# A two-layer decoder step: forget pages loaded as rows, SyncE in written order in the q/k stage, last outputs stored as whole rows

## The chip, the cores and the metric

The kernel runs on one NeuronCore of a Trainium2 chip. A core has five engines with instruction streams of their own: TensorE (PE in the profile, with its weight loads shown apart as PEld), VectorE (DVE), ScalarE (ACT), GpSimd (POOL) and SyncE (SP). SyncE computes nothing here: it issues DMA transfers and reads register values. ScalarE and GpSimd can issue transfers too, each on a queue of its own. The metric is the device time of one execution in microseconds; lower is better. The kernel before took 2829.18 us (median of 3 runs, 2827.18 to 2837.07).

## What is computed

One inference step of a two-layer decoder, for 1024 prompt tokens with 16 meta tokens ahead of them and for 8 decoding requests of 8 tokens each; all 1104 rows go through the same weights. Layer A is an mLSTM (a chunked recurrence with gates), layer B is attention in which every key carries a cumulated log-forget value. After each layer comes a SwiGLU network. Cut to what the change touches:

```python
def mlstm_mixer(xn, C0, n0, m0, lead, w_in, ...):
    p = xn @ w_in                       # q, k, v, output gate, and the small gates gi, gf
    q = heads(p[..., :HK], DK_A) * DK_A ** -0.5
    k = heads(p[..., HK:2 * HK], DK_A)
...
def attend_sample(q, k, v, lf):         # layer B, the 8 decoding requests
    lp = cache_logf[page_table].reshape(Bd, n_pages * PAGE_SIZE, H_B, ...)
    c = jnp.cumsum(jnp.concatenate([lp.astype(f32), lf], axis=1), axis=1)
...
y = rmsnorm(h, prm['norm_final'])       # the last output, y_prompt and y_sample
```

`cache_logf` has pages of 128 positions x 16 heads (8 KB in f32); the page table names 4 pages for each of 8 requests, so 32 pages are read. Everything is f32. A product is made of three passes of rounded halves (high x high, high x low, low x high), so every weight is split once into a high half (a copy on ScalarE that rounds) and a low half (a subtraction on VectorE).

## The kernel before

Work is written in stages that follow one another on TensorE. In stage A the input rows are turned and normalised and the values are made (`values_a`); then comes the **q/k stage** (in `phase_a`), then the recurrence with the output gates between its steps, the output projection and the first feed-forward network (`mlp`, `ffn`), then layer B in the same manner. The last step is in class `Tail`: three tiles of 128 rows remain whose output waits for the last product.

A planner lays out each engine's instruction stream from the program: it takes instructions by priority (written earlier comes first) as soon as by its own clock their data and buffers are there. A block `manual_schedule(engines={...})` takes the named engines out of that: their instructions written inside it keep the written order. The planner may still set others, which are written later, between them. At run time each stream is executed strictly in the order laid out, whatever the planner's clock had thought. In `values_a` (L648) TensorE, SyncE, VectorE and ScalarE are in written order; in the q/k stage before the change only TensorE is (L923).

The q/k stage (`qk_out`, L909 to L920) makes q and k for all rows: 8 blocks m of 128 columns, and in each three groups t of 336, 384 and 384 rows. One pass (m, t) is 24 matmuls (L193 to L195) into one of two PSUM banks, tag `mmA`; ScalarE copies the bank out (L918, tile `stg`) and GpSimd stores it to `qkD`. The passes are counted by x = 3 m + t, from 0 to 23. Between them, by x:

- `load_w` (L233) loads the 512 KB of weights of a block m (L256, tile `wraw`, two buffers) and splits them: high half on ScalarE (L259, `whi`), low half on VectorE (L260, `wlo`), three buffers each. Block 0 was loaded and split in `values_a` (`self.q0`).
- `wo_out` (x = 6, 9, 12, 15, 18) does the same with a block of the output projection's weights, and `wo_keep` stores the halves to `woD` on GpSimd's queue (L875), to be read back in `mlp`.
- `rec_prep` prepares the recurrence's gates. At x = 1 and x = 4 TensorE turns li and lf into rows (L1098, tag `r`, two PSUM banks, three turns each), ScalarE copies them out (L1100), and VectorE scans them (L1102 to L1132). At x = 9 TensorE turns the results back (L1140) and VectorE copies them (L1141).
- `cache_loads` (L997) reads the page table into `ptab` (L1001), and for each of the 32 pages reads its number into a SyncE register (L1008) and loads the page as 128 partitions x 64 bytes (L1010, tile `cp`). One step of it loads 4 pages; a step is taken after each x from 0.
- `cache_prep` (x = 14): 4 turns on TensorE (L1021), a copy with the sign changed on ScalarE (L1022), a scan along the positions on VectorE (L1024), and 8 stores to `csE` on GpSimd's queue (L1027). Layer B reads them much later.

In the functions below `wo_fetch` (L850) and `wo_split` (L859) are what `values_a` uses already: a load alone, and later the split alone.

In `Tail.out` (L2061), for each of three tiles, VectorE and ScalarE scale one half of 512 columns each out of PSUM into places of `net.H` that are 128 columns wide and 4 apart, and SyncE stores each half (L2072): six stores of 256 KB.

Of the kernel before, what the change touches and what calls it, by code (L numbers as in the profile page):

```python
# [8 lines left out]
F32 = mybir.dt.float32  # L9
F32R = mybir.dt.float32r  # L10
I32 = mybir.dt.int32
AF = mybir.ActivationFunctionType
ALU = mybir.AluOpType
# [4 lines left out]
P = 128  # L18
D = 1024
KT = D // P  # L20
NB, NQ = 8, 8
# [6 lines left out]
TT = [(0, T0)] + [(T0 + P * i, T0 + P * (i + 1)) for i in range(SEQ // P)]  # L28
# [10 lines left out]
HB, DH = 16, 64  # L39
DFF = 2816  # L40
NF = DFF // P
PAGE, NPG = 128, 4
PAST = PAGE * NPG
# [835 lines left out]
@_add(Net)  # L879
def phase_a(self, vt):  # L880
    nc, I, O = self.nc, self.I, self.O
    w_in = I["w_in_a"][0]
    qkD = self.dram.tile([8, P, T], F32, name="qkD")
    ogD = self.dram.tile([8, P, T], F32, name="ogD")
    v = lambda i: vt[:, i * HA * (DV + 1) : (i + 1) * HA * (DV + 1)].rearrange("p (h d) -> p h d", h=HA)
    with ExitStack() as c3:
        kp = c3.enter_context(self.pool("kA"))
        tm = kp.tile([P, NT, 104], F32, name="tmA")
        den = kp.tile([P, NT, HA], F32, name="den")
        ssq = kp.tile([P, NT, HA], F32, name="ssqA")  # L890
        self.C = [kp.tile([P, 4, DV + 1], F32, name=f"C{a}") for a in range(3)]
        gates = kp.tile([P, NT, 16], F32, name="gates")
        self.fin = (tm, den, ssq)
        for i in range(NT):
            nc.gpsimd.memset(v(i)[:, :, DV : DV + 1], 1.0)
        nc.gpsimd.memset(gates, 0.0)
        nc.gpsimd.memset(tm[:, 0, :], 0.0)
        nc.gpsimd.memset(den, 1.0)
        nc.gpsimd.memset(ssq, 1.0)
        st = c3.enter_context(self.pool("stA", bufs=3))  # L900
        self.woD, self.held = [], []
        self.values_a(v, kp, gates, w_in, c3)
        pp = c3.enter_context(self.pool("ppA", bufs=2, space=PSUM))

        def wo_out():
            m = len(self.woD)
            self.wo_keep(*self.load_w([I["w_out_a"][0][:, m * P : (m + 1) * P]]))

        def qk_out():  # L909

            for m in range(8):
                wh, wl = self.load_w([w_in[:, m * P : (m + 1) * P]]) if m else self.q0
                for t, (t0, t1) in enumerate(TG):
                    n = t1 - t0
                    ps = pp.tile([P, 512], F32, name=self.uid("mmA"), tag="mmA")
                    self.fm_cols(ps[:, :n], wh, wl, self.XG[t])
                    s = st.tile([P, GL], F32, name=self.uid("stg"), tag="stg")
                    nc.scalar.activation(s[:, :n], ps[:, :n], AF.Copy, scale=DK ** -0.5 if m < 4 else 1.0)  # L918
                    nc.gpsimd.dma_start(qkD[m, :, t0:t1], s[:, :n])
                    yield  # L920

        with self.pool("rowsA") as rp, self.pool("rowsAp", bufs=2, space=PSUM) as rpp, \
                self.pool("cp") as cp, self.tc.manual_schedule(engines={mybir.EngineType.PE}):  # L923
            pages = self.cache_loads(cp)
            prep = self.rec_prep(kp, gates, rp, rpp)
            next(prep)
            for x, _ in enumerate(qk_out()):
                if x in (1, 4, 9):
                    next(prep, None)
                next(pages, None)  # L930
                if x == 14:
                    self.cache_prep(*self.cache, rpp, "r")
                if x % 3 == 0 and 5 < x < 21:
                    wo_out()

        def gates_out():

            get = lambda m, later=None: self.load_w([w_in[:, (16 + m) * P : (17 + m) * P]], later=later)
            ws = [get(0)]
            later = []  # L940
            for m in range(8):
                wh, wl = ws[m]
                for t, (t0, t1) in enumerate(TG):
                    n = t1 - t0
                    ps = pp.tile([P, 512], F32, name=self.uid("mmA"), tag="mmA")
                    xh, xl = self.XG[t]
                    if t == 1 and m < 7:
                        ws.append(get(m + 1, later if m else None))
                    for k in range(KT):
                        if k == 6 and later:  # L950
                            later.pop()()
                        self.mm3(ps[:, :n], wh[:, k, :], wl[:, k, :], xh[:, k, :], xl[:, k, :], k == 0, k == KT - 1)
                        if k == KT - 1:
                            s = st.tile([P, GL], F32, name=self.uid("stg"), tag="stg")
                            nc.scalar.activation(s[:, :n], ps[:, :n], AF.Sigmoid)
                            nc.gpsimd.dma_start(ogD[m, :, t0:t1], s[:, :n])
                        yield

        left = {t: list(range(HA)) for t in range(3)}
        left[-1] = [None]  # L960

        def heads(pp, tag, op=None, some=None):

            ready, used = [], []
            todo = [(t, h) for t in (0, 1, 2) for h in left[t]][:some]

            def ahead():
                if todo:
                    t, h = todo.pop(0)
                    og = op(self.uid("ogc")) if callable(op) else op.pop(0)  # L970
                    nc.gpsimd.dma_start(og[:, : TG[t][1] - TG[t][0]], ogD[h, :, TG[t][0] : TG[t][1]])
                    ready.append(og)

            def gate(t):
                if not left[t]:
                    return False
                while todo and (len(ready) < 3 if callable(op) else op):
                    ahead()
                if t < 0:
                    return False  # L980
                og = ready.pop(0)
                self.gate_head(t, left[t].pop(0), v, og, pp, tag)
                if not callable(op):

                    used.append(og)
                    if len(used) > 1:
                        op.append(used.pop(0))
                return True
            return gate

        self.recurrence(kp, self.rec, v, qkD, gates_out(),
                        lambda places: heads(pp, "mmA", places, 10))
    return heads


@_add(Net)
def cache_loads(self, cp):  # L997

    nc, I = self.nc, self.I
    self.csE = self.dram.tile([NB, P, PAST], F32, name="csE")  # L1000
    nc.sync.dma_start(self.ptab, I["page_table"].rearrange("b n -> (b n)").unsqueeze(0))  # L1001
    self.pages = []
    a, b = (cp.tile([P, 2 * PAST], F32, name=f"cp{x}") for x in range(2))
    lp = a[:, : NPG * NB * HB].rearrange("p (n b h) -> p n b h", n=NPG, b=NB)
    for b_ in range(NB):
        for n in range(NPG):
            j = b_ * NPG + n
            v = nc.sync.value_load(self.ptab[0:1, j : j + 1], min_val=0, max_val=I["cache_k"].shape[0] - 1)  # L1008
            self.pages.append(v)
            nc.sync.dma_start(lp[:, n, b_, :], I["cache_logf"][bass.DynSlice(v, 1)].rearrange("a p h -> (a p) h"))  # L1010
        yield
    self.cache = lp, a[:, PAST:], b[:, :PAST], b[:, PAST:]


@_add(Net)
def cache_prep(self, lp, cs, lt, on, pp, tag):

    nc = self.nc
    ps = pp.tile([P, 512], F32, name="csps", tag=tag)
    for n in range(NPG):  # L1020
        nc.tensor.transpose(ps[:, n * P : n * P + P], lp[:, n].rearrange("p b h -> p (b h)"), self.ident)  # L1021
    nc.scalar.activation(lt, ps, AF.Copy, scale=-1.0)  # L1022
    nc.gpsimd.memset(on, 1.0)
    nc.vector.tensor_tensor_scan(cs, on, lt, 0.0, ALU.mult, ALU.add)  # L1024
# [977 lines left out]
class Tail:  # L2002
# [57 lines left out]

    def out(self, x, lo, hi):  # L2061
        net, i = self.net, DONE[3][x]
        nc, t0, t1 = net.nc, *TT[i]
        for g, ps in enumerate((lo, hi)):
            o = net.H[:, 4 * g : 4 * g + 4, t0:t1]
            y, rr = ps.rearrange("p (k n) -> p k n", k=4), self.r[:, 1, x : x + 1]
            if g:
                nc.scalar.activation(o, y, AF.Copy, scale=rr)
            else:
                nc.vector.scalar_tensor_tensor(out=o, in0=y, scalar=rr, in1=net.sq[:, :512].rearrange(  # L2070
                    "p (k n) -> p k n", k=4), op0=ALU.mult, op1=ALU.mult)
            nc.sync.dma_start(net.O["y_prompt"][0, (i - 1) * P : i * P, g * 512 : g * 512 + 512].rearrange(  # L2072
                "p (k n) -> p k n", k=4), o)

    def finish(self, acc, groups):
        net = self.net
# [963 lines left out]
```

## Time and profile before

| | us |
|---|---|
| median of 3 runs | 2829.18 (2827.18 to 2837.07) |
| profiled execution, its own time | 2829.72 |
| its span (first to last instruction) | 2828.0 |
| TensorE busy in the span | 2761.9 (98%) |
| VectorE, ScalarE, GpSimd busy | 1800.4, 1177.3, 836.0 |
| mean granted TensorE clock | 0.994 |

The page shows one profiled execution. Busy times are sums over the span; matmuls are pipelined, so that a busy TensorE is not one at its peak, and where it is slowed by its clock only the granted clock tells so. "DMA" is the mean busy share of 16 DMA engines. In a timeline each row has the start, the length, the engine, the source line, the operation, what it writes and reads, how many were merged, and in brackets how long the engine had stood idle before and what ended that. A row of "who waited" has the waiting group, the releasing one, the sum in us, the number of times and the longest. Rows of a table by windows have the window, its length, each engine's busy time with its number of instructions, the granted clock, the DMA share and GB/s.

### The profile page before, as it was taken

The page shows a single profiled execution, that of the slowest core. Times are in us where ns is not written, and L with a number is a line of the kernel's source. Part 1 is how long each engine was busy: PE and PEld are TensorE (multiplying, and loading weights), DVE is VectorE, ACT ScalarE, POOL GpSimd, SP SyncE. Part 2 cuts the span into 40 slices and gives each one's busy share as a digit, 9 for nine tenths or more (in the row PEclk, how much of TensorE's full clock was granted, in tenths as well). Part 3 has the DMA queues.
Part 4 walks back from the last instruction along what each step waited for, and adds up shares of the span by engine and source line. Part 5 has one row for each costly group of instructions (what it writes and reads, how often), then busy time and mean ns, then how long its engine had stood idle before and what let it go on. Part 6 is the DMA issues. An engine that isn't in the chain of part 4 may idle for free. (4 is left out here: it accounts for less than half of the span.)

```text
span 2828.0 us, 60538 instructions
## 1 busy us (share of the span) xinstructions
PE 2761.9 (98%) x23543; PEld 2650.3 (94%) x23543; DVE 1800.4 (64%) x4025; ACT 1177.3 (42%) x2299; POOL 836.0 (30%) x1313
## 2 busy tenths in 40 slices
PE   8999999999999999999999999999999999999998
PEld 8989889999999999999999888677999999999998
DVE  4632566888887765563455444777388888766556
ACT  5422453432322334443444445777343223323345
POOL 3122233132232332124453202544313223323111
PEclk9999999999999999999999999999999999999999
DMA  6666547245554375545444676442524555527556
GB/s 196 171 196 162 144 125 255 90 143 165 176 167 148 112 243 174 195 145 171 139 172 132 237 279 226 154 143 86 157 83 128 175 176 164 161 90 239 178 191 215
DMA packets 439001, 474.03 MB, mean 168 GB/s; under 512 B 41422, under 2 KB 365258, under 8 KB 437690
## 3 DMA queue, kind: packets, MB, share of 16 engines
q1 hardware_dynamic: 387522, 320.78, 36.8%
q0 software_dynamic: 43808, 143.17, 15.3%
q10 hardware_dynamic: 7384, 6.22, 0.7%
q8 instruction: 185, 3.03, 0.5%
q14 instruction: 102, 0.84, 0.1%
HBM read 322.84 MB, written 147.21 MB: 166 GB/s over the span
## 5 line engine op out<-in xcount | busy, mean ns | idle before, releaser
L1611 PE MATMUL m<-xh,slot 128*128 128x276 f32 x2752 | 541.3, 290 | 1.8 <-ACT fs L1640 1.8
L1611 PEld LDWEIGHTS m<-xh,slot 128*128 128x128 f32 x2752 | 440.4, 188 | 3.6 <-ACT fs L1640 2.2
L1611 PE MATMUL m<-xl,slot 128*128 128x276 f32 x1376 | 397.4, 289 | 0.0
L1611 PEld LDWEIGHTS m<-xl,slot 128*128 128x128 f32 x1376 | 259.1, 188 | 0.0
L193 PE MATMUL tmps<-slot,xh 128*128 128x256 f32 (+2 forms) x864 | 243.1, 281 | 0.0
L195 PE MATMUL tmps<-slot,xl 128*128 128x256 f32 (+2 forms) x864 | 240.6, 278 | 0.0
L194 PE MATMUL tmps<-slot,xh 128*128 128x256 f32 (+2 forms) x864 | 240.5, 278 | 0.0
L272 DVE TENSOR_TENSOR slot<-slot,slot 128x1024 fp32r<-128x1024 f32 x124 | 162.9, 1314 | 60.7 <-ACT slot L271 59.2
L271 ACT CAST slot<-slot 128x1024 fp32r<-128x1024 f32 x124 | 129.6, 1046 | 141.2 <-PE m L1611 111.7
L194 PEld LDWEIGHTS tmps<-slot,xh 128*128 128x128 f32 (+1 forms) x864 | 159.2, 184 | 0.1
L195 PEld LDWEIGHTS tmps<-slot,xl 128*128 128x128 f32 (+1 forms) x864 | 158.6, 184 | 0.0
L193 PEld LDWEIGHTS tmps<-slot,xh 128*128 128x128 f32 (+1 forms) x864 | 158.4, 183 | 0.2
L193 PE MATMUL mmA<-xh,whi 128*128 128x384 f32 (+1 forms) x384 | 135.1, 352 | 0.0
L194 PE MATMUL mmA<-xl,whi 128*128 128x384 f32 (+1 forms) x384 | 127.9, 333 | 0.0
L195 PE MATMUL mmA<-xh,wlo 128*128 128x384 f32 (+1 forms) x384 | 127.7, 333 | 0.0
L272 DVE TENSOR_TENSOR slot<-vA,slot 128x1024 fp32r<-128x1024 f32 (+1 forms) x59 | 82.2, 1396 | 32.6 <-ACT slot L271 31.5
L272 DVE TENSOR_TENSOR slot<-Ht,slot 128x1024 fp32r<-128x1024 f32 (+1 forms) x59 | 81.4, 1382 | 32.3 <-ACT slot L271 31.1
L271 ACT CAST slot<-Ht 128x1024 fp32r<-128x1024 f32 (+1 forms) x59 | 61.0, 1037 | 96.8 <-PE m L1611 92.9
L271 ACT CAST slot<-vA 128x1024 fp32r<-128x1024 f32 (+1 forms) x59 | 60.8, 1035 | 95.5 <-PE m L1611 90.5
L1715 DVE TENSOR_TENSOR ws<-ws 128x128 f32<-128x128 f32 x264 | 93.8, 355 | 8.9
L2862 ACT ACTIVATE s<-s,nb 128x272 f32<-128x272 f32 (+7 forms) x126 | 98.9, 786 | 0.0
L2897 ACT COPY th<-tp 128x768 f32<-128x768 f32 (+1 forms) x80 | 73.6, 920 | 53.7 <-PE tp L2889 30.5
(805 smaller groups left out, 8668.8 us busy)
## 6 DMA issues: line engine op xcount, KB each, us to landing
ws<-in_w_down SPq DMA_DIRECT2D x176, 128.0 KB, 2.8
sD<-ws SPq DMA_DIRECT2D x176, 128.0 KB, 2.3
slot<-sD SPq DMA_DIRECT2D x40, 512.0 KB, 4.2
slot<-in_w_gate_up SPq DMA_DIRECT2D x36, 512.0 KB, 3.9
kp<-in_cache_k SPq DMA_DIRECT2D x32, 512.0 KB, 6.7
vp<-in_cache_v SPq DMA_DIRECT2D x32, 512.0 KB, 5.1
vA<-in_w_gate_up SPq DMA_DIRECT2D x26, 512.0 KB, 4.4
Ht<-in_w_gate_up SPq DMA_DIRECT2D x26, 512.0 KB, 3.9
```

What stands on the lines that cost most here:

```text
L193: mm(ps, sh, mh, start=first, stop=False)
L194: mm(ps, sh, ml, start=False, stop=False)
L195: mm(ps, sl, mh, start=False, stop=last)
L271: self.nc.scalar.copy(hi, src)
L272: self.nc.vector.tensor_tensor(out=lo, in0=src, in1=hi.bitcast(F32), op=ALU.subtract)
L1611: nc.tensor.matmul(u.ps[h, b], w[p][:, k], x[q][:, k], start=first and k == i == 0, stop=k == 3 and i == 2, skip_group_check=True)
L1715: tt(out=o, in0=a, in1=b, op=ALU.subtract)
L2862: nc.scalar.activation(ss[z, u], ss[z, u], AF.Exp, bias=nb[:, z : z + 1], accum_out=sm[:, u, z : z + 1])
L2897: nc.scalar.copy(th.rearrange("p x z (u h q) -> p h (x z u) q", h=2, q=64)[:, :, :n], pt[:, :, :n])
```

## The change

Three things are edited.

**Pages.** `cache_loads` loads a page as one row of 8 KB into one partition of a tile `pg` (32 rows used), instead of 128 pieces of 64 bytes. `cache_prep` then first turns the 16 heads' columns on TensorE (16 turns of 32 rows into 128, out of steps of 16 elements) into one PSUM bank, VectorE copies the bank with its order changed to `lp`, and the 4 turns follow as before. It comes at x = 12 instead of 14. The pages' steps begin at x = 1.

**SyncE.** In the q/k stage SyncE is in written order as well as TensorE. Weights come by `wo_fetch` and `wo_split`: the load of q/k block m + 1 is written at (m, 0), ahead of its matmuls, that of output block m + 2 at (m, 1) for m from 1 to 5; the splits are written at (m, 2), and at (m, 0) for the output block. The written order on SyncE is so: block 1; page table; pages of 8; block 2; pages of 4; output block 3; pages of 8; block 3; pages of 4; output block 4; pages of 8; block 4, and so on without pages. Reading the page numbers into registers stands in that order too, each ahead of its page.

**Last outputs.** `Tail.out` writes both halves of a tile side by side into one row of `net.H` (1024 columns) and stores the tile with one transfer of 512 KB with rows of 4 KB; the third of the three is issued by ScalarE instead of SyncE.

```diff
@@ -879,6 +879,7 @@
 @_add(Net)
 def phase_a(self, vt):
     nc, I, O = self.nc, self.I, self.O
+    E = mybir.EngineType
     w_in = I["w_in_a"][0]
     qkD = self.dram.tile([8, P, T], F32, name="qkD")
     ogD = self.dram.tile([8, P, T], F32, name="ogD")
@@ -902,36 +903,37 @@
         self.values_a(v, kp, gates, w_in, c3)
         pp = c3.enter_context(self.pool("ppA", bufs=2, space=PSUM))
 
-        def wo_out():
-            m = len(self.woD)
-            self.wo_keep(*self.load_w([I["w_out_a"][0][:, m * P : (m + 1) * P]]))
-
         def qk_out():
 
             for m in range(8):
-                wh, wl = self.load_w([w_in[:, m * P : (m + 1) * P]]) if m else self.q0
+                wh, wl = self.q0
                 for t, (t0, t1) in enumerate(TG):
+                    if t == 0 and m < 7:
+                        self.wo_fetch(w_in[:, (m + 1) * P : (m + 2) * P])
+                    elif t == 1 and 0 < m < 6:
+                        self.wo_fetch(m + 2)
                     n = t1 - t0
                     ps = pp.tile([P, 512], F32, name=self.uid("mmA"), tag="mmA")
                     self.fm_cols(ps[:, :n], wh, wl, self.XG[t])
                     s = st.tile([P, GL], F32, name=self.uid("stg"), tag="stg")
                     nc.scalar.activation(s[:, :n], ps[:, :n], AF.Copy, scale=DK ** -0.5 if m < 4 else 1.0)
                     nc.gpsimd.dma_start(qkD[m, :, t0:t1], s[:, :n])
+                    if t == 2 and m < 7 or t == 0 and len(self.held) > 1:
+                        self.wo_split()
                     yield
 
         with self.pool("rowsA") as rp, self.pool("rowsAp", bufs=2, space=PSUM) as rpp, \
-                self.pool("cp") as cp, self.tc.manual_schedule(engines={mybir.EngineType.PE}):
+                self.pool("cp") as cp, self.tc.manual_schedule(engines={E.PE, E.SP}):
             pages = self.cache_loads(cp)
             prep = self.rec_prep(kp, gates, rp, rpp)
             next(prep)
             for x, _ in enumerate(qk_out()):
                 if x in (1, 4, 9):
                     next(prep, None)
-                next(pages, None)
-                if x == 14:
+                if x:
+                    next(pages, None)
+                if x == 12:
                     self.cache_prep(*self.cache, rpp, "r")
-                if x % 3 == 0 and 5 < x < 21:
-                    wo_out()
 
         def gates_out():
 
@@ -1000,25 +1002,32 @@
     self.csE = self.dram.tile([NB, P, PAST], F32, name="csE")
     nc.sync.dma_start(self.ptab, I["page_table"].rearrange("b n -> (b n)").unsqueeze(0))
     self.pages = []
-    a, b = (cp.tile([P, 2 * PAST], F32, name=f"cp{x}") for x in range(2))
-    lp = a[:, : NPG * NB * HB].rearrange("p (n b h) -> p n b h", n=NPG, b=NB)
-    for b_ in range(NB):
+    raw = cp.tile([P, PAGE * HB], F32, name="pg")
+    for b in range(NB):
         for n in range(NPG):
-            j = b_ * NPG + n
+            j = b * NPG + n
             v = nc.sync.value_load(self.ptab[0:1, j : j + 1], min_val=0, max_val=I["cache_k"].shape[0] - 1)
             self.pages.append(v)
-            nc.sync.dma_start(lp[:, n, b_, :], I["cache_logf"][bass.DynSlice(v, 1)].rearrange("a p h -> (a p) h"))
+            nc.sync.dma_start(raw[n * NB + b : n * NB + b + 1, :],
+                              I["cache_logf"][bass.DynSlice(v, 1)].rearrange("a p h -> a (p h)"))
         yield
-    self.cache = lp, a[:, PAST:], b[:, :PAST], b[:, PAST:]
-
-
-@_add(Net)
-def cache_prep(self, lp, cs, lt, on, pp, tag):
+    self.cache = raw, cp.tile([P, PAST], F32, name="lp")
+
+
+@_add(Net)
+def cache_prep(self, raw, lp, pp, tag):
 
     nc = self.nc
+    J = NB * NPG
+    ps = pp.tile([P, 512], F32, name="pgps", tag=tag)
+    for h in range(HB):
+        nc.tensor.transpose(ps[:, h * J : h * J + J], raw[:J].rearrange("j (t h) -> j t h", h=HB)[:, :, h],
+                            self.ident[:J, :J])
+    nc.vector.tensor_copy(lp.rearrange("p (j h) -> p j h", h=HB), ps.rearrange("p (h j) -> p j h", h=HB))
+    cs, lt, on = (raw[:, x * PAST : (x + 1) * PAST] for x in range(3))
     ps = pp.tile([P, 512], F32, name="csps", tag=tag)
     for n in range(NPG):
-        nc.tensor.transpose(ps[:, n * P : n * P + P], lp[:, n].rearrange("p b h -> p (b h)"), self.ident)
+        nc.tensor.transpose(ps[:, n * P : n * P + P], lp[:, n * P : n * P + P], self.ident)
     nc.scalar.activation(lt, ps, AF.Copy, scale=-1.0)
     nc.gpsimd.memset(on, 1.0)
     nc.vector.tensor_tensor_scan(cs, on, lt, 0.0, ALU.mult, ALU.add)
@@ -2060,17 +2069,11 @@
 
     def out(self, x, lo, hi):
         net, i = self.net, DONE[3][x]
-        nc, t0, t1 = net.nc, *TT[i]
-        for g, ps in enumerate((lo, hi)):
-            o = net.H[:, 4 * g : 4 * g + 4, t0:t1]
-            y, rr = ps.rearrange("p (k n) -> p k n", k=4), self.r[:, 1, x : x + 1]
-            if g:
-                nc.scalar.activation(o, y, AF.Copy, scale=rr)
-            else:
-                nc.vector.scalar_tensor_tensor(out=o, in0=y, scalar=rr, in1=net.sq[:, :512].rearrange(
-                    "p (k n) -> p k n", k=4), op0=ALU.mult, op1=ALU.mult)
-            nc.sync.dma_start(net.O["y_prompt"][0, (i - 1) * P : i * P, g * 512 : g * 512 + 512].rearrange(
-                "p (k n) -> p k n", k=4), o)
+        nc, rr = net.nc, self.r[:, 1, x : x + 1]
+        y = net.H[:, x, :D]
+        nc.scalar.activation(y[:, 512:], hi, AF.Copy, scale=rr)
+        nc.vector.scalar_tensor_tensor(out=y[:, :512], in0=lo, scalar=rr, in1=net.sq[:, :512], op0=ALU.mult, op1=ALU.mult)
+        (nc.scalar if x == 2 else nc.sync).dma_start(net.O["y_prompt"][0, (i - 1) * P : i * P], y)
 
     def finish(self, acc, groups):
         net = self.net
```

## The prediction

> **What bounds the kernel now.** I read the page's slices first, then who TensorE waited for in the q/k stage, and a table of windows of that stage.
>
> ```profile
> PE   8999999999999999999999999999999999999998
> ```
>
> ```profile
> core 0: us, PE busy (x) PEld busy (x) DVE busy (x) ACT busy (x) POOL busy (x), PEclk, DMA share, GB/s
> 126.72:245.00 118.28, 111.01 (x671) 109.03 (x669) 39.36 (x76) 33.46 (x53) 27.43 (x58) 0.96 0.67 195
> 155.55:158.70 3.15, 3.15 (x11) 2.98 (x12) 3.15 (x10) 0.78 (x2) 1.11 (x2) 0.50 0.61 168
> 158.70:161.85 3.15, 3.15 (x20) 3.15 (x20) 3.15 (x3) 0.10 (x1) 0.00 (x0) 1.00 0.23 66
> 177.17:181.04 3.87, 3.67 (x27) 3.13 (x25) 1.43 (x3) 1.22 (x2) 0.55 (x1) 1.00 1.08 391
> 182.50:185.91 3.41, 3.41 (x13) 3.41 (x12) 1.23 (x1) 0.00 (x0) 0.00 (x0) 0.51 0.70 183
> 186.00:189.41 3.41, 3.41 (x21) 3.41 (x21) 0.00 (x0) 0.49 (x1) 0.55 (x1) 1.00 0.53 159
> ```
>
> ```profile
> PE rps L1098 <- ACT lf L1100: 6.8, 1, 6.8
> PE wps L1144 <- DVE tmA L1141: 0.2, 1, 0.2
> ```
>
> TensorE bounds the kernel nearly everywhere. The q/k stage (126.7 to 245) leaves it idle for 7.3 us of 118.3, almost all in one wait of 6.8 us, and twice its clock is halved for about 3 us. Who held the wait up is told by the timelines of TensorE, ScalarE and SyncE:
>
> ```profile
> 147.96 0.78 PE L1098 MATMUL rps<-ident,lf_tm 80*8 80x80 f32 x6
> 155.55 0.80 PE L1098 MATMUL rps<-ident,lf_tm 128*8 128x128 f32 x3 [6.80 <-ACT lf L1100]
> 156.00 0.67 PE L193 MATMUL mmA<-xh,whi 128*128 128x384 f32 x1
> ```
>
> ```profile
> 153.75 1.04 ACT L259 CAST whi<-wraw 128x1024 fp32r<-128x1024 f32 x1 [9.25 <-DMA wraw<-in_w_in_a]
> 154.70 0.48 ACT L918 ACTIVATE stg<-mmA 128x384 f32<-128x384 f32 x1
> 155.08 0.78 ACT L1100 COPY lf<-rps 8x336 f32<-8x336 f32 x2
> ```
>
> ```profile
> 122.86 2.64 SPq L256 DMA_DIRECT2D wraw<-in_w_in_a  x2
> 130.71 0.37 SPq L256 DMA_DIRECT2D wraw<-in_w_out_a  x1
> 131.34 18.28 SPq L1010 DMA_DIRECT2D cp<-in_cache_logf  x32
> 149.74 0.39 SPq L256 DMA_DIRECT2D wraw<-in_w_in_a  x1
> ```
>
> Read from below: SyncE issued all 32 pages in one piece, 18.28 us, and block 3's weight load behind them, at 149.74. ScalarE had that block's split next in its stream and stood 9.25 us for it, although TensorE's pass x = 4 had been over since 147.96. Behind it queued the copy of that pass and the first copy of lf, whose PSUM bank the third turn of lf needs. TensorE did not need block 3 itself for another three passes.
>
> **The change part by part.** The sum is made against the profiled execution, 2829.72 us (span 2828.0 and 1.7 around it), 0.5 us above the median of 2829.18.
>
> **1. The wait.** If it goes, 6.8 us go. Behind it 11 matmuls fill 3.15 us at a clock of 0.50 where the next 3.15 us hold 20; those from 156.00 to 158.70 would take about half of 2.7 us: 1.3 us more. **−8.1 us**; bounds 0 and −8.1.
>
> Whether it goes hangs on when block 3 lands and where the planner puts its split. The register reads are a cost here that the stage did not have: the planner had set them into the values stage, and now they stand in SyncE's written order, each ahead of its page.
>
> ```profile
> L1008 SPq TENSOR_LOAD <-ptab x32: 262/275/1086, 12.7 to 47.3; - x32
> L1008 SPq FUSED_REGOPS  x32: 147/147/181, 13.2 to 47.6; - x32
> L1008 SPq SEQ_ASSERT  x32: 18/18/33, 13.4 to 47.8; - x32
> L1001 SPq DMA_DIRECT2D ptab<-in_page_table x1: 289/289/289, 8.2 to 8.2; - x1
> DMA to landing us min/median/max: 1.5/1.7/4.0
> DMA to landing us min/median/max: 4.2/4.8/5.5
> ```
>
> (The first landing row is the pages', the second the weights'.) A page costs 0.57 us of issuing (18.28 / 32) and 0.44 for its number (0.275 + 0.147 + 0.018): 1.01 us; one row of 8 KB in place of 128 pieces I price the same, since the page table, one piece, still takes 0.29 to issue. Block 3 now stands behind block 1, the page table (0.29 and its landing, 1.7 as a page), 20 pages, block 2 and one output block: 122.9 + 0.4 + 2.0 + 20.2 + 0.8 = 146.3, landed 4.8 later at 151. That is only 2 to 3 us earlier than the 153.75 of today, and with the page table's 4.5 us of the start (8.2 to 12.7) it isn't earlier at all. So the gain doesn't come from an earlier load. It comes from ScalarE's order: the split must be laid out behind the copies that are due at 148 to 149. Today the planner had reckoned with 32 cheap issues; now its clock has to count 20 register reads as well, which it set one after another into SyncE's idle stretches before, so it prices them as something. I take it that the split falls behind the lf copies. A split that then waits till 151 delays only the copy of x = 5, due at about 153. Nothing else is late: block 4, behind all 32 pages (122.9 + 2.4 + 32.3 + 2.0), is issued at about 160 and landed at 165, and x = 12, which needs it, begins two passes behind the turns of x = 9, which begin at 177 today and 169 then; a pass of 24 matmuls is 3.8 us at 20 in 3.15.
>
> **2. The turns.** TensorE has 16 more of them, out of 32 rows. The nearest row:
>
> ```profile
> L1140 PE MATMUL tps<-ident,stk x9: 251/252/309, 177.2 to 178.1; 104*128 104x104 f32 x8, 104*80 104x104 f32 x1
> 177.17 1.18 PE L1140 MATMUL tps<-ident,stk 104*80 104x104 f32 x9
> L1141 DVE COPY tmA<-tps x3: 263/592/592, 177.5 to 178.4; 128x416 f32<-128x416 f32 x2, 80x104 f32<-80x104 f32 x1
> L1021 PE MATMUL csps<-ident,cp x4: 270/272/272, 203.1 to 203.4; 128*128 128x128 f32 x4
> ```
>
> 9 in 1.18 us are 0.13 each, so 16 take **+2.1 us** on TensorE itself; bounds 1.6 (weights alone, at 0.1) and 4.2 (twice, for columns read at steps of 16).
>
> **3. The copy between the turns.** The 4 old turns read what VectorE copies after the 16 new ones, so TensorE, whose order is written, stands meanwhile, and pass x = 13 behind it. 128x416 took 0.592, so 128x512 takes 0.73, with 0.2 on each side for the hand-over (TensorE waited 0.2 for L1141 above): **+1.1 us** if VectorE is free. Bounds 0.7 (the copy alone) and 6.5, if VectorE's stream has a weight split ahead that waits for a store, as here:
>
> ```profile
> 198.80 1.23 DVE L260 TENSOR_TENSOR wlo<-wraw,whi 128x1024 fp32r<-128x1024 f32 x1 [5.41 <-DMA woD<-wlo]
> ```
>
> **4. The clock.** 16 turns, the copy and 4 turns (0.6 us) are 3.8 us of light work. The windows show what followed 3.87 us of it at x = 9 (turns and tiny products): 3.41 us at clock 0.51, with 13 matmuls where 21 fit, a loss of 1.3 us. **+1.3 us**; bounds 0 and 1.3. The Trainium skill, "TensorE: Matmul & The Clock Gate", Part 4, says that turns do not count as busy for the gate; by it the 3.8 us is idle to the gate and the loss sure, without it only the 1.1 us wait would count and the loss could be nothing.
>
> **5. The tail.** What is left of the kernel after TensorE's last product:
>
> ```profile
> 2819.96 4.12 SPq L2072 DMA_DIRECT2D out_y_prompt<-Ht  x6
> L2070 DVE SCALAR_TENSOR_TENSOR Ht<-fin,tr,sq 128x512 f32<-128x512 f32 x3 | 2.1, 744 | 0.1
> 24.00:30.00 6.00, 5.13 (x45) 4.97 (x44) 4.76 (x11) 5.02 (x12) 0.86 (x1) 1.00 1.02 393
> 2821.00:2826.50 5.50, 0.00 (x0) 0.00 (x0) 0.38 (x1) 0.09 (x1) 0.00 (x0) 0.51 0.99 281
> DMA packets 654, 2.36 MB, mean 393 GB/s; under 512 B 78, under 2 KB 79, under 8 KB 653
> DMA packets 3169, 1.58 MB, mean 122 GB/s; under 512 B 96, under 2 KB 3168, under 8 KB 3168
> ```
>
> The 16 DMA engines are full (0.99) from 2821.0 to 2826.5, at 281 GB/s, in pieces under 2 KB (the second packet row). In the stretch of the first packet row, 24 to 30, nearly all were 2 to 8 KB and the same engines, as full, moved 393. The 1.57 MB in rows of 4 KB then take 4.0 us. They start later, since a store needs both halves: about 2820.1 instead of 2819.96. The tiles are ready each 0.7 us and need 1.3 to move, so the engines don't starve, and the issue on ScalarE's queue saves nothing that is on the path: **−1.4 us**; bounds −1.6 and +0.2 (no faster rate). The Trainium skill, "DMA: Bandwidth & Descriptors", Specifications, puts line rate at 512 B and more; by it the rate would stay and the tail come out at +0.2, but the two windows speak against it. It is a rival below.
>
> **6. The values stage** loses SyncE's 32 register reads.
>
> ```profile
> 27.80 1.06 PE L732 MATMUL xps<-ident,xin 128*128 128x128 f32 x8 [0.86 <-DMA xin<-in_x_prompt]
> 32.36 0.52 PE L193 MATMUL tmps<-whi,xh 128*80 128x272 f32 x1 [1.99 <-ACT whi L271]
> ```
>
> The input loads between 17 and 33 stand among them. I take **−0.5 us**, half of the wait of 0.86 for an input; bounds 0 and −2.9 (both waits).
>
> At no cost: GpSimd's queue issues the same transfers, with the stores to `csE` two passes earlier, where TensorE waits for none of them (the only waits of the stage are those above), and the weights' splits are the same instructions.
>
> The sum is −8.1 + 2.1 + 1.1 + 1.3 − 1.4 − 0.5 = −5.5 us: 2829.7 − 5.5 = 2824.2, 0.5 less on the scale of the median; I say **2824**.
>
> **The rivals.**
>
> *The wait stays (slower).* The planner still lays block 3's split ahead of the lf copies, which decides it. As block 3 lands at 151 to 154, ScalarE stands as today and part 1 is worth nothing: −5.5 + 8.1 = +2.6, 2832.3 us. For it: the landing by the sum above has hardly moved. Against it: the split is written at x = 8 and the copies at x = 4, and only a clock that runs ahead of SyncE's real pace lets it in.
>
> *A new wait in place of the old.* VectorE's copy of the pages stands behind a weight split that waits for its store (5.41 + 1.23 above): TensorE stands up to 5.4 us longer at x = 12, 2829.6 us, as before. For it: VectorE waited so at 198.8, close to where x = 12 ends. Against it: the copy is written before the next split.
>
> *The stores are no faster.* Issue or memory limits them, not the size of a piece: 1.6 us more, 2825.8.
>
> *The planner lays out other streams anew.* Engines not in written order may change places anywhere behind. The largest idle sum that it could touch is layer B's:
>
> ```profile
> 1580.00:1980.00 400.00, 380.99 (x4773) 304.36 (x4771) 227.38 (x1008) 254.54 (x494) 134.13 (x339) 1.00 0.56 192
> ```
>
> 19 us of 400. All of it gone would make 2805, as much again 2843. Nothing in the trace speaks for either.
>
> **How the numbers follow.** Forecast 0.47, the wait stays 0.16, the new wait 0.12, stores no faster 0.05, other streams 0.20 (gain and loss even). A measurement of this kernel can tell about 0.5% from no change, 14 us: below 2815.0 or above 2843.3. Only the last case reaches that far, with half of its 0.20 each way at most; a forecast with its best bounds (turns 1.6, copy 0.7, no clock loss, −2.9 in the values stage) gives 2819.4, and the first rival with a late copy and no faster stores 2839. So faster 0.10, same 0.80, slower 0.10. The range takes in these bounds but for the far ends of the last case: 2815 to 2836.
>
> **What would show it.** Right: no wait of TensorE for ScalarE's lf copies; a row of 16 turns, a gap of about 1.1 us and 4 turns between x = 12 and 13; clock 0.5 for 3.4 us after it, none at 156; the last three stores moving at about 390 GB/s for 4 us; register reads on SyncE from 123 to 165. Wrong: a wait of 5 us or more at L1098 (first rival) or at L1021's turns (second); stores at 281 GB/s; or gains and losses beyond 245 us that no part names.

## The result and the profile after

The changed kernel takes 2849.47 us (median of 5 runs) where the kernel before took 2832.84 beside it (5 runs): ratio 1.0068, 95% interval 1.0057 to 1.008. It is slower by 0.7%. The profiled execution is 2848.91 us with a span of 2846.9, against 2829.72 and 2828.0 before: 18.9 us more of span.

Start times of the same TensorE instruction in the two traces (in pass x; m is the block) tell where they went; the lag is after minus before:

| instruction | before | after | lag | in between |
|---|---|---|---|---|
| last lf turn begins | 155.55 | 149.35 | -6.2 | wait for lf gone |
| x = 5 under way | 158.39 | 150.90 | -7.5 | its half-clock gone |
| x = 6 under way (m = 2) | 163.33 | 166.85 | +3.5 | waits of 8.65 and 0.33, half-clock |
| x = 9 under way (m = 3) | 176.56 | 186.35 | +9.8 | waits of 2.51 and 0.88, half-clock |
| x = 12 begun (m = 4) | 191.37 | 205.75 | +14.4 | waits of 1.56 and 0.69; the half-clock behind the turns of x = 9 lasts 6.8 us (clock 0.50 and 0.58 from 191.27 to 198.07), twice as long as before |
| x = 13 begun | 194.74 | 214.40 | +19.7 | 16 and 4 turns, wait of 2.73 |
| x = 13 under way | 196.30 | 217.26 | +21.0 | half-clock |
| near the end | 2757.69 | 2777.97 | +20.3 | 18.7 to 22.4 all along |

All of the loss arises between 150 and 220 us. First the view of who TensorE waited for in 126.7 to 245 (sum, times, longest), after the window row of the same stretch (the row of before had a clock of 0.96 and 671 matmuls):

```profile
126.70:245.00 118.30, 100.05 (x548) 95.63 (x547) 40.13 (x77) 29.31 (x46) 24.98 (x55) 0.88 0.56 169
```

```profile
PE mmA L193 <- ACT whi L271: 12.7, 3, 8.6
PE csps L1030 <- DVE lp L1026: 2.7, 1, 2.7
PE mmA L195 <- DVE wlo L272: 1.9, 3, 0.9
PE rps L1107 <- ACT lf L1109: 0.3, 1, 0.3
162.66 0.65 PE L193 MATMUL mmA<-xh,whi 128*128 128x336 f32 x1 [8.65 <-ACT whi L271]
```

The wait that bound the kernel before, 6.8 us for lf, is 0.3. In its place TensorE waits three times for a weight block's split (`whi`, `wlo`), the first time for 8.65 us ahead of x = 6 (last line), and once for the copy between the turns. ScalarE's and SyncE's timelines show why, for block 2:

```profile
148.89 0.78 ACT L1109 COPY lf<-rps 8x336 f32<-8x336 f32 x2
155.13 1.12 ACT L1136 ACTIVATE stk<-mA 8x1104 f32<-8x1104 f32 x1 [4.78 <-DVE mA L1119]
156.27 0.49 ACT L919 ACTIVATE stg<-mmA 128x384 f32<-128x384 f32 x1
159.01 1.12 ACT L1133 ACTIVATE wA<-wA 8x1104 f32<-8x1104 f32 x1 [2.24 <-DVE wA L1131]
160.41 1.12 ACT L1143 ACTIVATE stk<-bA 8x1104 f32<-8x1104 f32 x1 [0.29 <-DVE bA L1141]
161.56 1.04 ACT L271 CAST whi<-wraw 128x1024 fp32r<-128x1024 f32 x1
```

```profile
129.52 9.26 SPq L1011 DMA_DIRECT2D pg<-in_cache_logf  x8
138.88 0.41 SPq L854 DMA_DIRECT2D wraw<-in_w_in_a  x1
...
145.88 9.60 SPq L1011 DMA_DIRECT2D pg<-in_cache_logf  x8
163.89 0.41 SPq L854 DMA_DIRECT2D wraw<-in_w_in_a  x1
```

Block 2's load was issued at 138.88. Its split at 161.56 has no bracket: ScalarE did not wait for the data. It had stood idle for 4.78 and 2.24 us for VectorE's scans just before, with the split laid out behind the three exps that need those scans. So the weight was late by its place in ScalarE's stream. The delay then reaches SyncE: two raw buffers hold the blocks, so block 3's load, which SyncE reached at 155.5 (145.88 + 9.60), went out at 163.89, when block 2's split had been done.

The tail came out near its forecast. From the start of the last group of products to the end of the span it takes 8.17 us (2838.73 to 2846.9) in place of 9.44 (2818.56 to 2828.0):

```profile
2840.29 0.99 SPq L2076 DMA_DIRECT2D out_y_prompt<-Ht  x2
2841.62 0.36 ACTq L2076 DMA_DIRECT2D out_y_prompt<-Ht  x1
2841.00:2845.00 4.00, 0.00 (x0) 0.00 (x0) 0.53 (x1) 0.25 (x1) 0.00 (x0) 0.73 0.98 393
```

393 GB/s with the DMA engines full (0.98), as the prediction had it, against 281 before.

### The profile page after: what moved, and what is told of

Same layout as the page of the kernel before. It is cut to its first block, busy times and chain, and to the rows that moved or that the text cites. A ratio compares the mean times of both kernels' runs of the same rounds, so it can differ in the third digit from the quotient of the medians.

```text
span 2846.9 us, 60569 instructions
## 1 busy us (share of the span) xinstructions
PE 2772.1 (97%) x23559; PEld 2657.5 (93%) x23559; DVE 1797.6 (63%) x4026; ACT 1176.5 (41%) x2299; POOL 833.9 (29%) x1313
## 5 line engine op out<-in xcount | busy, mean ns | idle before, releaser
L193 PE MATMUL mmA<-xh,whi 128*128 128x384 f32 (+1 forms) x384 | 138.1, 360 | 12.8 <-ACT whi L271 12.7
## 6 DMA issues: line engine op xcount, KB each, us to landing
ws<-in_w_down SPq DMA_DIRECT2D x176, 128.0 KB
sD<-ws SPq DMA_DIRECT2D x176, 128.0 KB
```

The costliest lines, as they stand in the source:

```text
L193: mm(ps, sh, mh, start=first, stop=False)
```

## The experiments

Two theories for the late splits. **Theory 1**: the planner, which lays out ScalarE's and VectorE's streams, reckons the rows of 8 KB as slow, so it takes every weight behind them on SyncE for late and sets its split late. **Theory 2**: the register reads, now in SyncE's written order, make the loads really late. A third, that the written order of SyncE as such does it, goes with the second. The lag in the table is that of the same TensorE instruction against before, at 300 us of before, in the profiled runs; the changed kernel's lag there is 21.5. Differences of 1.5 us between lags are no finding: between 258 and 261 us the kernel before has a stretch of half clock that `tail`, for one, does not have, and that alone moves its lag by 1.4.

| kernel | median us | ratio to before, 95% | lag at 300 | TensorE's waits over 1 us, 126.7 to 245 |
|---|---|---|---|---|
| tail | 2828.41 | 0.9984 to 1.0004 | -1.3 | lf 7.2 |
| pages | 2833.89 | 1.0004 to 1.0024 | +3.9 | VectorE's tmA 4.0, whi 1.6 |
| order | 2833.89 | 1.0001 to 1.0021 | +3.0 | stg 8.3 |
| free | 2833.38 | 1.0005 to 1.0024 | +4.4 | whi 1.6 twice, stg 2.0, lp 1.2 |
| early | 2842.92 | 1.0032 to 1.0063 | +16.8 | whi 3.7, 1.6, 1.6, wlo 3.8, lp 2.8 |
| late | 2851.08 | 1.0063 to 1.0096 | +24.6 | page rows 10.2 |
| reads | 2824.31 | 0.9974 to 0.9992 | -4.4 | li 1.5 |
| shift | 2820.19 | 0.996 to 0.9982 | -8.8 | none |
| turns | 2823.64 | 0.9972 to 0.9991 | -3.2 | none |
| moved | 2840.96 | 1.0028 to 1.0058 | +13.2 | page rows 12.8, whi 1.6 |
| hand | 2839.25 | 1.0018 to 1.005 | +10.5 | stg 6.1 and 2.3, lf 1.3, li 1.2 |
| hand2 | 2829.52 | 0.9993 to 1.0013 | +2.8 | stg 2.7 (at 234), lf 1.3, li 1.2 |

**tail**: the kernel before with the new `Tail.out` alone.

> The kernel before with the new last stores alone. If a store's rate hangs on the size of its pieces, the last 1.57 MB move at 390 to 410 GB/s and the end comes 1.4 us earlier: span 2826.6 in place of 2828.0, all of it after 2819, nothing changed in the q/k stage. If the tail also costs something that the trace of the changed kernel hides elsewhere, the ratio comes out above 1.

The q/k stage is as before (wait of 7.2 us for lf). The tail took 8.22 us (2819.98 to 2828.2), 1.2 less than before, moving 397, 397 and 426 GB/s in the three full microseconds. The span, 2828.2, did not fall, because TensorE was 1.4 us later at 2809 by small differences that came and went through both layers; the interval holds both 1 and 0.9995.

**order**: the changed kernel with the functions `cache_loads` and `cache_prep` of before.

```diff
-            nc.sync.dma_start(raw[n * NB + b : n * NB + b + 1, :],
-                              I["cache_logf"][bass.DynSlice(v, 1)].rearrange("a p h -> a (p h)"))
+            nc.sync.dma_start(lp[:, n, b_, :], I["cache_logf"][bass.DynSlice(v, 1)].rearrange("a p h -> (a p) h"))
```

> The changed kernel with the pages loaded and turned as before (64-byte pieces, 4 turns): SyncE's written order, the loads and splits of weights apart, the register reads in line and the new stores stay. Theory 1 (the planner prices the loads of whole rows dearly, takes the weights behind them for late and lays their splits late in ScalarE's stream): without rows the splits stand early, no wait of TensorE for whi over 1 us in the q/k stage, and the old wait for lf is gone: 2820 to 2824 us where the kernel before takes 2830. Theory 2 (the register reads on SyncE make the weights late): the waits at blocks 2 and 3 stay, 2838 us or more. Theory 3 (SyncE's written order as such): the same 2838 or more.

Neither was right as a whole. Waits for whi are gone, as theory 1 had it, with the reads still in line. But the time is not 2822: a new wait of 8.3 us for a copy of PSUM (`stg`) stands at 165.4. ScalarE's and SyncE's timelines of this kernel:

```profile
140.90 1.05 ACT L271 CAST whi<-wraw 128x1024 fp32r<-128x1024 f32 x1 [4.79 <-DMA wraw<-in_w_in_a]
149.36 0.47 ACT L1102 COPY lf<-rps 8x384 f32<-8x384 f32 x1 [0.21 <-PE rps L1100]
162.68 1.04 ACT L271 CAST whi<-wraw 128x1024 fp32r<-128x1024 f32 x1 [12.85 <-DMA wraw<-in_w_in_a]
```

```profile
128.68 8.32 SPq L1012 DMA_DIRECT2D cp<-in_cache_logf  x8
137.11 0.40 SPq L854 DMA_DIRECT2D wraw<-in_w_in_a  x1
153.30 0.39 SPq L854 DMA_DIRECT2D wraw<-in_w_in_a  x1
```

With pieces of 64 bytes block 2 is split at 140.90, not at 161.56, although its load went out at nearly the same time (137.11, not 138.88). Now block 3's split stands early too, right behind the lf copies, and its load goes out at 153.30 only: ScalarE stands 12.85 us for it, the same kind of wait as before the change, two passes further on (ahead of x = 7, not x = 5). So theory 1 holds for block 2, and the reads have a price of their own.

**reads**: `order` with the page table's load and all 32 reads written ahead of the stage.

```diff
+        self.page_numbers()
         with self.pool("rowsA") as rp, self.pool("rowsAp", bufs=2, space=PSUM) as rpp, \
...
-            v = nc.sync.value_load(self.ptab[0:1, j : j + 1], min_val=0, max_val=I["cache_k"].shape[0] - 1)
-            self.pages.append(v)
+            v = self.pages[j]
```

> The kernel `order` (pages as 64-byte pieces and 4 turns, SyncE in written order, new last stores) with the page table's load and the register reads written ahead of the stage. If the reads in line are what made block 3's load late there (issued at 153.3, split at 162.7, TensorE 8.3 us behind it), it is issued 12 to 14 us earlier, at about 140, the wait goes and the time is 2820 to 2823 us, ratio 0.997. If the pages' pieces hold the weights' transfer up, the wait stays over 4 us: 2827 or more.

```profile
140.65 0.39 SPq L854 DMA_DIRECT2D wraw<-in_w_in_a  x1
146.28 1.05 ACT L271 CAST whi<-wraw 128x1024 fp32r<-128x1024 f32 x1 [0.20 <-DMA woD<-whi]
150.12 0.78 ACT L1109 COPY lf<-rps 8x336 f32<-8x336 f32 x2
PE rps L1107 <- ACT li L1109: 1.5, 1, 1.5
```

Block 3's load is issued 12.65 us earlier (140.65), the wait is gone, and the kernel is faster than before. Without the reads the split also has another place: at 146.28, ahead of the lf copies (150.12), where in `order` it stood behind them. The time, 2824, is a little above the forecast; 1.5 us of it is a wait for li at 137.

**early**: the changed kernel with the reads written ahead in the same way, rows and turns kept.

> The changed kernel with the page table's load and the 32 register reads written ahead of the q/k stage: SyncE's written order holds the row loads and the weights' loads alone. Theory 2 (the reads in line make the weights late): no wait for whi over 1 us is left, 2826 to 2830 us. Theory 1 (the planner prices the row loads dearly and lays the weights' splits late): the loads come earlier, but block 2's split is still laid behind the copy of pass x = 5, and block 3's behind that of x = 8: waits of 2 to 5 us for whi at both places, 2836 to 2844 us.

```profile
129.61 0.41 SPq L854 DMA_DIRECT2D wraw<-in_w_in_a  x1
155.46 0.49 ACT L919 ACTIVATE stg<-mmA 128x384 f32<-128x384 f32 x1
155.85 1.04 ACT L271 CAST whi<-wraw 128x1024 fp32r<-128x1024 f32 x1
156.94 0.65 PE L193 MATMUL mmA<-xh,whi 128*128 128x336 f32 x1 [3.74 <-ACT whi L271]
161.64 0.65 PE L195 MATMUL mmA<-xh,wlo 128*128 128x336 f32 x1 [3.77 <-DVE wlo L272]
```

Theory 2 falls here: with no reads in the stage, block 2's load goes out at 129.61, nine microseconds earlier than in the change, and its split still stands behind the copy of pass x = 5, at 155.85, 26 us later. VectorE's half of the split stands behind its scans as well. As pieces against rows is the only difference in loads between `reads` (2824) and `early` (2843), rows move the splits. (With the rows come 16 turns and a copy, but these are written far behind block 2's split, at x = 12, and in `turns` below, which has them without rows, no split is waited for.)

**free** (the changed kernel, `engines={E.PE}`) and **pages** (the kernel before with rows, turns and nothing else).

> The changed kernel with SyncE left to the planner in the q/k stage (only TensorE in written order). Theory 1 (the planner's price of the rows): block 2's split is early again, so the wait of 8.65 us at 162.7 goes, but block 3's split stays behind the copy of pass x = 8 and TensorE waits 2 to 5 us for it; the turns and their clock loss stay: 2835 to 2842 us. Theory 2 or 3 (the reads, or the written order): no wait for whi over 1 us is left, 2822 to 2828 us.

> The kernel before with the new page loads and turns alone: no written order on SyncE, weights loaded and split together as before, cache_prep at x = 14, old last stores. Theory 1 (the planner's price of the rows): a split of block 2 or 3 is laid late and TensorE waits for it 2 to 9 us; with the 16 turns, the copy and the clock after them (5 us) the time is 2835 to 2845. Theory 2 or 3 (the reads in line, or the written order): no such wait, the time is that of before plus the turns' 4 to 5 us at most, 2828 to 2835 us.

In both the planner put block 2's load ahead of the rows on SyncE, and block 2 was split in time; block 3's split stood behind the copy of x = 8 and cost 1.6 + 0.7 us (in `free` block 4's as much again). The times lie a little below theory 1's ranges, since 2 to 5 us were expected for that wait; for `free` they are well above the 2822 to 2828 of theory 2, while `pages` by its time alone fits both and is told by its wait for whi. So SyncE's written order is not needed for a late split of block 3. It is what put rows ahead of block 2, and the other 17 us of lag (21.5 against 4.4) came with it.

**late** and **moved**: the changed kernel with the page steps behind all weights (x = 19 to 22), or from x = 6 on (the edit shown is that of `moved`).

```diff
-                if x:
+                if x > 5:
                     next(pages, None)
-                if x == 12:
+                if x == 14:
```

> The changed kernel with the page rows loaded behind all weights of the stage (8 a step at x = 19 to 22, cache_prep at x = 23). Theory 1 and theory 2 both: the splits stand early in ScalarE's stream again and land early, so no wait of TensorE for whi over 1 us and none for lf; what is left of the change's cost is the turns, the copy and the clock after them (4 to 5 us), against 8 us gained and 1.4 in the tail: 2822 to 2827 us. If the turns cost more than that by themselves, or the late rows hold layer B up, 2830 or more.

> The changed kernel with the page steps taken from x = 6 on in place of x = 1, and cache_prep at x = 14: block 2's and block 3's loads are written ahead of all rows, block 4's behind 12 of them, block 5's behind 24. Theory 1 (the planner lays late the split of whatever weight is written behind the rows): no wait for whi at x = 6 and x = 9, but one of 2 to 5 us at x = 12 and one at x = 15, since their splits now stand late: 2834 to 2842 us. Theory 2 (only the real lateness of the loads counts): block 4 is issued at about 165 and block 5 at 180, landed 12 and 8 us before they are needed, so no wait for whi over 1 us anywhere: 2824 to 2828 us.

In these two the rows themselves came too late, which neither theory had priced. In `late`, SyncE needs 1.32 us for each row with its read in line. No split is waited for in the stage, as both theories said, and TensorE is 7.0 us ahead of before at 196. At the turns it waits 10.2 us for rows and, behind the stage, 13.4 for a state that queues behind them:

```profile
198.20 42.34 SPq L1012 DMA_DIRECT2D pg<-in_cache_logf  x32
PE n0p L1325 <- DMA n<-in_state_n: 13.4, 1, 13.4
```

In `moved` the waits at x = 6 and 9 are gone and one for a split appears at x = 12, as theory 1 had it (1.56 and 0.68 us, not 2 to 5); the one at x = 15 doesn't. The time falls into theory 1's range mostly by a wait of 12.8 us for rows. These were late by the same cause: block 4, loaded at 155.75, was split at 185.63 only, with no idle time of ScalarE's just ahead of it, and SyncE, in its written order, stood from 174.7 to 187.95 for that block's raw buffer, with 8 rows still behind.

```profile
155.75 0.41 SPq L854 DMA_DIRECT2D wraw<-in_w_in_a  x1
163.45 11.28 SPq L1011 DMA_DIRECT2D pg<-in_cache_logf  x8
187.95 0.41 SPq L854 DMA_DIRECT2D wraw<-in_w_in_a  x1
185.63 1.04 ACT L271 CAST whi<-wraw 128x1024 fp32r<-128x1024 f32 x1
```

**shift**: the kernel before with the new `Tail.out` and the page steps from x = 6 on.

```diff
-                next(pages, None)
+                if x > 5:
+                    next(pages, None)
                 if x == 14:
```

> The kernel before with the new last stores and the page steps taken from x = 6 on in place of x = 0, nothing else: the weights of blocks 2 and 3 pass ahead of most pages on SyncE. If the wait for lf of the kernel before hangs on block 3's load standing behind 32 pages alone, it goes with its clock loss: 2820 to 2823 us, ratio 0.997. If it hangs on ScalarE's order alone, it stays: 2828 us.

```profile
138.52 0.39 SPq L256 DMA_DIRECT2D wraw<-in_w_in_a  x1
144.25 1.05 ACT L259 CAST whi<-wraw 128x1024 fp32r<-128x1024 f32 x1
126.70:245.00 118.30, 117.25 (x716) 114.13 (x716) 43.33 (x84) 35.05 (x55) 28.79 (x59) 0.99 0.71 202
```

Block 3's load goes out at 138.52 instead of 149.74, its split at 144.25 waits for nothing, TensorE is busy for 117.25 of 118.3 us at a clock of 0.99. At 2820.19 us, ratio 0.9971 (0.996 to 0.9982), it is the fastest of all, faster than both kernels. The old wait hung on where the load stood on SyncE: ScalarE's split stands ahead of the lf copies here as it did before. (The planner set 12 pages ahead of block 3's load all the same, not 32.)

**turns**: `shift` with the 16 turns and the copy between, on zeros, so that the sums of the pages are left out.

> The kernel `shift` with the 16 turns and VectorE's copy between them and the 4 turns, all on a tile of zeros that is in place long before (the pages' sums are not computed from the pages here). It prices the turns by themselves, with no row load in the stage. By the sum of the prediction: turns 2.1, copy and hand-over 1.1, clock 1.3, together 4.5 us in the profile above `shift` (span 2817.3), so 2821 to 2822 of span, ratio to the kernel before 0.9985. If a split of VectorE stands ahead of the copy, up to 2 us more.

```profile
195.16 1.94 PE L1025 MATMUL pgps<-ident,t 32*128 32x32 f32 x16
197.88 0.81 PE L1030 MATMUL csps<-ident,t 128*128 128x128 f32 x4 [0.78 <-DVE t L1027]
198.40:201.80 3.40, 3.40 (x15) 3.40 (x14) 1.94 (x3) 1.65 (x2) 1.08 (x2) 0.52 0.68 176
201.80:205.20 3.40, 3.40 (x22) 3.40 (x22) 0.35 (x1) 0.45 (x1) 3.19 (x6) 1.00 1.04 386
```

The turns take 1.94 us, the copy's wait 0.78, and 3.4 us at half clock follow, 15 matmuls where 22 fit. TensorE against `shift` goes from -0.55 at the first turn (195.16 against 195.71) to +3.73 at the last slow matmul (201.57 against 197.84): 4.3 us, against 4.5 forecast.

**hand**: the changed kernel with ScalarE in written order and the split one pass earlier.

```diff
-                    if t == 2 and m < 7 or t == 0 and len(self.held) > 1:
+                    if t == 1 and m < 7 or t == 0 and len(self.held) > 1:
                         self.wo_split()
...
-                self.pool("cp") as cp, self.tc.manual_schedule(engines={E.PE, E.SP}):
+                self.pool("cp") as cp, self.tc.manual_schedule(engines={E.PE, E.SP, E.Activation}):
```

> The changed kernel with ScalarE in written order too in the q/k stage, and the split of the next block written one pass earlier (behind the second pass of a block in place of the third). Rows, reads in line and SyncE's order stay as they are; only the place of the splits in ScalarE's stream is taken from the planner. Theory 1 (the planner lays the splits late, the weights themselves are there in time): no wait for whi over 1 us at x = 6 and x = 9, the turns' 4 to 5 us stay: 2824 to 2831 us. Theory 2 (the reads and rows make the loads really late): ScalarE stands for the loads instead and TensorE with it, 5 us or more at x = 6 or 9: 2838 us or more.

No wait for a split is left, so the weights were there in time. But the written order put the three exps ahead of the copies of passes 5 and 6, and TensorE waited 6.1 us for one of those: a time in theory 2's range by a cause that it doesn't have. **hand2** takes that away:

```diff
+            yield
             nc.scalar.activation(w, w, AF.Exp)
...
-                if x in (1, 4, 9):
+                if x in (1, 4, 6, 9):
```

> The kernel `hand` with the three exps of rec_prep written behind pass x = 6 in place of x = 4, so that they no longer stand ahead of the copies of passes 5 and 6 in ScalarE's written order (TensorE waited 6.1 us for one of these there). Everything that the change adds stays: rows, turns, register reads in SyncE's written order. Theory 1 (in the changed kernel it is the place of the splits in ScalarE's stream that costs the time): neither whi nor stg is waited for longer than 1 us at x = 6 to 9; with the turns' 4 to 5 us and the gain at lf: 2824 to 2832 us. Theory 2 (the weights come too late behind rows and reads): a wait of 3 us or more at x = 6 or 9 stays in one form or another, 2836 us or more.

```profile
149.67 1.04 ACT L271 CAST whi<-wraw 128x1024 fp32r<-128x1024 f32 x1
166.70 1.05 ACT L271 CAST whi<-wraw 128x1024 fp32r<-128x1024 f32 x1 [1.22 <-DMA wraw<-in_w_in_a]
169.07 0.42 PE L195 MATMUL mmA<-xh,wlo 128*128 128x336 f32 x1 [0.68 <-DVE wlo L272]
```

Block 2 is split at 149.67, block 3 at 166.70, just in time (0.68 us at x = 9). Block 2's load went out at 139.10 here, as in the changed kernel (138.88), so its data were there by 149.67 and not just by 161.56. With all that the change adds still in it, the kernel takes 2829.52 us, a ratio of 1.0003 in place of 1.0068: the loss is gone by the places of the splits and the exps. These are not ScalarE's alone, since VectorE's half of a split is written earlier with it (block 2's at 150.73, in the changed kernel at 162.64). That the time is not the forecast's goes in part to waits that ScalarE's written order brings, for li, lf and stg. What is left of theory 2 is small: SyncE's issue of block 3 at 155.44 leaves ScalarE 1.22 us short.

## Why the prediction was wrong

The forecast was 2824 with a range to 2836. The measured 2849.47 lies beyond it and on the slower side, which had 0.10.

**1, the wait: right in itself, wrong beside it.** It goes (6.8 to 0.3) with its clock loss, -7.5 us within x = 5 against -8.1. The split of block 3 did fall behind the lf copies, as "I take it that the split falls behind the lf copies" said. (TensorE needed that block four passes after the old wait, x = 5 to 8, not three as the prediction has it.) The failed step is the sentence that follows from it, "Nothing else is late", together with "the weights' splits are the same instructions" at no cost. The argument that moves block 3's split back moves that of every weight behind pages on SyncE, and block 2, which has 8 rows ahead of it in the written order, was not looked at. That alone turned -7.5 into +3.5; blocks 3 and 4 followed for lack of raw buffers and by the same placing. The cause was put too narrowly: "its clock has to count 20 register reads". The reads do move block 3's split as it said, from ahead of the lf copies (`reads`) to behind them (`order`). But rows, which it priced like pieces, move splits further: block 2's stands ahead of the copy of x = 2 with reads and pieces (`order`), and behind that of x = 5 with rows and no reads (`early`). What figure the planner gives a row no trace tells; that it is this figure that decides is argued from the layouts.

The reads were also undercounted as a real cost. A page was to take 1.01 us of SyncE; with its read it took 1.2 (9.60 for 8) to 1.32 (42.34 for 32), and with the table's load the first read began at 128.0 and the first page at 129.5, 6.4 us after block 1's load, where 2.4 were allowed. In `order` block 3's load so went out at 153.30 instead of 146.3, and that cost 8.3 us.

**2 and 4, the turns and the clock:** 1.94 against 2.1; half clock for 3.4 us behind the turns, as in part 4. The Trainium skill's rule named there ("TensorE: Matmul & The Clock Gate", Part 4) agrees with `turns`: the only wait was 0.78 us and the clock still fell to 0.52. A wait like that does not do it by itself: behind one of 0.81 us at 124.02 in the kernel before the clock was 1.00 up to 127.40.

**3, the copy:** alone 0.78 of wait against 1.1. In the changed kernel it was 2.73, as VectorE had a split ahead of it: a mild form of the second rival, inside the bounds of 0.7 and 6.5.

**5, the tail:** -1.25 (8.17 to 8.22 us against 9.44), against -1.4, at the rate forecast. The rival by the Trainium skill's rule, no faster stores, falls.

**6, the values stage:** nothing instead of -0.5. TensorE was 0.56 us ahead at 28 to 35 and 0.28 behind from 37 on.

**The rivals.** None was this. The one called "the planner lays out other streams anew" was put in layer B, with gain and loss even; it happened in the stage itself. For block 2, which TensorE needs first, a split that moves back can only lose, and the price stood in the trace of before, in ScalarE's timeline behind the wait: 4.90 us of idle time for VectorE's scan ahead of the first exp, with a later split (162.91) between the exps.

```profile
161.75 1.13 ACT L1127 ACTIVATE stk<-mA 8x1104 f32<-8x1104 f32 x1 [4.90 <-DVE mA L1110]
162.91 1.05 ACT L259 CAST whi<-wraw 128x1024 fp32r<-128x1024 f32 x1
166.66 1.13 ACT L1124 ACTIVATE wA<-wA 8x1104 f32<-8x1104 f32 x1 [0.79 <-DVE wA L1122]
```

A split moved behind these three is held by VectorE, whenever its data lands.

## What to carry to other kernels

An edit that changes the form of a transfer can also move the consumers of everything queued behind it: before pricing such a change, list each load behind it on that queue, and ask where its consumer goes in every stream that is not in written order. A split that shows no idle time ahead of it, long after its load went out, is late by its place and not by its data; what helped here was to move the load ahead of the others (`shift`, one line in the kernel before) or to write the split's place by hand (`hand2`); making those others cheaper did not.

## What the runs showed of the hardware

The same register read on SyncE took longer in the q/k stage of the changed kernel (median 488 ns, first line) than in the values stage of the kernel before (275 ns):

```profile
L1009 SPq TENSOR_LOAD <-ptab x32: 453/488/1557, 128.0 to 191.0; - x32
126.27 3.24 SPq L1018 DMA_DIRECT2D pg<-in_cache_logf  x8
123.85 5.21 SPq L1019 DMA_DIRECT2D cp<-in_cache_logf  x8
```

Without reads in line a row of 8 KB took 0.41 us to issue (3.24 / 8, second line, from `early`) and a page in 64-byte pieces 0.65 (5.21 / 8, third line, from `reads`); the later runs of rows and pieces in the same two traces took 0.38 to 0.56 and 0.50 to 0.84. Why the reads take longer there was not tried.
